# Rotary embedding and q·kᵀ in fp32 on one core: the last eight rows of five GpSimd loads move to other DMA engines

## The chip, the cores and the metric

The kernel runs on one core of a Trainium2 chip. The metric is device time in microseconds (us) of one execution. The core has a tensor engine (PE, with its weight loads shown as PEld), a vector engine (DVE), a scalar engine (ACT), GpSimd (POOL), and SyncE (SP), which here only issues transfers. Sixteen DMA engines move data between HBM and the on-chip memory; the code numbers them 0 to 15, and so does this text (E0 to E15).

## The reference

Inputs are `q` and `k` of shape (16, 512, 16, 64) in fp32 (batch, sequence, heads, dimension) and `cos`, `sin` of shape (512, 32). Both `q` and `k` are rotated, then multiplied for each position and each head of one batch against all positions of the same batch and head:

```python
q_rot = np.concatenate([q1 * cos_q - q2 * sin_q, q1 * sin_q + q2 * cos_q], axis=-1)
k_rot = np.concatenate([k1 * cos_q - k2 * sin_q, k1 * sin_q + k2 * cos_q], axis=-1)
scores = np.einsum('bshd,bthd->bsht', q_rot, k_rot)
```

`q1`, `q2` are the first and second half of the 64 columns, and `cos_q`, `sin_q` are spread over batch and heads. The output has shape (16, 512, 16, 512): 268.4 MB are written, 67.2 MB read.

## The kernel before

A batch of `q` or `k` is 512 positions of 1024 numbers (16 heads of 64). It is laid in a tile of 128 partitions ("rows" below), four positions to a row, so a row is 16 KB and a batch 2 MB. `in_pool` has two buffers for `q` and two for `k`. The work goes in 64 steps, four to a batch (`i // 4` is the batch). In step `i`, for each of eight pairs of heads, PE makes the scores of 128 positions against 512 (line 201), ACT copies them from PSUM to the tile `st` (line 208), and after the eighth pair SP stores `st`, 4 MB, to `out` (line 188). Three buffers `st` rotate. Beside it DVE rotates the next positions of `q` and `k` in place (lines 149, 150, 154), PE transposes them through PSUM (line 170), and DVE or ACT copies them out (line 185).

Batch 0 and the first loads come in smaller pieces (the tile `early`). From step 4 on the kernel loads whole batches: at the end of each step with `i % 4 == 2` the `q` of the next batch but one, at the end of each with `i % 4 == 3` the `k` of the batch three ahead, in `load` (lines 113 to 122). Most loads are one transfer of 128 rows of 16 KB that SP issues (line 122), between its stores, so that each DMA engine gets eight rows.

Five loads go around one DMA engine: those named in `RELIEVED`, `q` of batches 6, 11 and 15 and `k` of batches 7 and 12. `SLOW = 4` names the engine that is passed over. GpSimd issues their first 120 rows (line 98) as descriptors that are dealt out from a cursor: fifteen engines from E5 on, round to E3, get eight rows each, in two halves of 8 KB (the access pattern takes the second half first, so that a row stays two pieces). The cursor stands where the last GpSimd transfer left it; it is reset once (line 101) and moved by tiny reads into `scratch` of as many rows as the cursor is to move (`move_cursor`, line 84). The last eight rows go in one of two ways. For the three loads of `q`, SP issues them (line 111) as eight rows of 16 KB, one to each of E0 to E7. For the two loads of `k`, GpSimd issues them first (line 98, called from line 107), with the cursor at 8, so one row to each of E8 to E15.

The order of each engine's instructions is the order in which they are written. GpSimd does nothing else after the first microseconds: its transfers wait for the tile to come free (PE's last transpose from it), and, as eight completion semaphores go round among GpSimd's transfers, a transfer also waits until the one eight places before it has landed.

Of the kernel before, what the change touches and what calls it, by code (L numbers as in the profile page):

```python
# [10 lines left out]
def kernel(  # L11
# [8 lines left out]
    nc = tc.nc  # L20
    fp32 = mybir.dt.float32
# [3 lines left out]
    B, S, H, D = q.shape  # L25
    HD = D // 2
    P = 128
# [5 lines left out]
    const_pool = ctx.enter_context(tc.tile_pool(name="const", bufs=1))  # L33
# [37 lines left out]
    batches = {}  # L71

    RELIEVED = {("q", 6): 0, ("k", 7): 1, ("q", 11): 2, ("k", 12): 3, ("q", 15): 4}
    SLOW = 4
    scratch = const_pool.tile([P, 96], fp32, name="scratch")
    tiny = [0]

    def move_cursor(n):

        y = tiny[0]
        tiny[0] += 1
        src = bass.AP(q.tensor, 512 * y, [(512, n), (64, 2), (1, 2)])
        nc.gpsimd.dma_start(scratch[:n, 4 * y : 4 * y + 4].rearrange("p (a b) -> p a b", a=2), src)

    def load_around(which, b, t):

        n, E, F = 120, C * H * D, C * H * D // 2  # L90
        x = RELIEVED[which, b]
        d = dram[which][b]

        def halves(lo, hi):
            src = bass.AP(d.tensor, d.offset + lo * E + F, [(E, hi - lo), (-F, 2), (1, F)])
            v = t[lo:hi].rearrange("p c e -> p (c e)")
            dst = bass.AP(v.tensor, v.offset + F, [v.ap[0], (-F, 2), (1, F)])
            nc.gpsimd.dma_start(dst, src)  # L98

        if x == 0:  # L100
            nc.gpsimd.inc_swdge_sem([], [], mode="reset_dge_cursor")
        else:

            move_cursor(16 - SLOW)
        if x % 2:
            move_cursor(8)
            halves(n, P)
        move_cursor(SLOW + 1)
        halves(0, n)
        if not x % 2:  # L110
            nc.sync.dma_start(t[n:].rearrange("p c (h d) -> p c h d", h=H), d[n:])

    def load(which, b):

        if b >= B:
            return
        t = in_pool.tile([P, C, H * D], fp32, tag=which + "_in", name=which + "_sb")
        batches[which, b] = t
        if (which, b) in RELIEVED:
            load_around(which, b, t)  # L120
        else:
            nc.sync.dma_start(t.rearrange("p c (h d) -> p c h d", h=H), dram[which][b])
# [100 lines left out]
    with tc.manual_schedule():  # L223
# [15 lines left out]
        for i in range(C):  # L239
# [7 lines left out]
            for p in range(HP):  # L247
# [7 lines left out]
                if p in (2, 6):  # L255
                    m = len(dve) - (4 if p == 2 else 2) - (2 if i == C - 1 else 0)
# [64 lines left out]
```

## Time and profile before

| | |
|---|---|
| median of 4 runs | 792.83 us (791.71 to 793.74) |
| the profiled execution | 792.68 us |
| its span, first to last instruction | 790.9 us |
| mean granted PE clock | 0.936 |
| busy share of PE / ACT / DVE / POOL | 86% / 71% / 69% / 2% |
| moved by SP's queue (q1) | 325.46 MB in 16704 packets |
| moved by GpSimd's queue (q0) | 10.10 MB in 1808 packets |

The profile page gives the busy time of each engine and, for the DMA engines, the mean share of time that their packets took. The trace keeps more than the page: every packet with start, duration, size and queue (not the DMA engine that carried it), and every increment of a transfer's semaphore. A transfer raises its semaphore sixteen times, once as each engine ends its part, so the sixteen times of one transfer show how far apart the engines are. The engines work off SP's transfers in the order in which they were issued. As an engine's next packet starts within some nanoseconds of the end of the one before, the packets can also be strung together into sixteen chains, one for each engine.

### The profile page before, as it was taken

The page shows a single profiled execution, that of the slowest core. Times are in us where ns is not written, and L with a number is a line of the kernel's source. Part 1 is how long each engine was busy: PE and PEld are TensorE (multiplying, and loading weights), DVE is VectorE, ACT ScalarE, POOL GpSimd, SP SyncE. Part 2 cuts the span into 40 slices and gives each one's busy share as a digit, 9 for nine tenths or more (in the row PEclk, how much of TensorE's full clock was granted, in tenths as well). Part 3 has the DMA queues.
Part 4 walks back from the last instruction along what each step waited for, and adds up shares of the span by engine and source line. Part 5 has one row for each costly group of instructions (what it writes and reads, how often), then busy time and mean ns, then how long its engine had stood idle before and what let it go on. Part 6 is the DMA issues. An engine that isn't in the chain of part 4 may idle for free.

```text
span 790.9 us, 7750 instructions
## 1 busy us (share of the span) xinstructions
PE 683.9 (86%) x3072; PEld 295.0 (37%) x3072; DVE 544.5 (69%) x516; ACT 561.1 (71%) x647; POOL 12.0 (2%) x24
## 2 busy tenths in 40 slices
PE   4999998997989989798897978989899698799960
PEld 2444443343433434343343433334343243344420
DVE  7999987576865778575785856767678477587400
ACT  3888886785857778486785856768587586588770
POOL 0000000000001000000000001000000000000000
PEclk9999999898998999899998989999899899899995
DMA  9999999999999999999999999999999999999997
GB/s 358 419 426 438 428 438 429 423 441 431 427 427 430 421 432 411 439 423 432 440 423 434 437 427 426 424 430 430 430 431 424 439 433 427 426 435 428 433 435 315
DMA packets 18836, 336.18 MB, mean 425 GB/s; under 512 B 2312, under 2 KB 3592, under 8 KB 4616
## 3 DMA queue, kind: packets, MB, share of 16 engines
q1 hardware_dynamic: 16704, 325.46, 96.3%
q0 software_dynamic: 1808, 10.10, 3.1%
q8 instruction: 24, 0.39, 0.2%
q10 hardware_dynamic: 288, 0.13, 0.1%
q14 instruction: 12, 0.10, 0.0%
HBM read 67.24 MB, written 268.44 MB: 424 GB/s over the span
## 4 chain that ended last, share of the span: by engine, by line
DMA 46%; PE 38%; DVE 7%; ACT 5%; issue 1%; ACTq 0%
DMA out_dram<-st 46%; PE ps L201 29%; PE bank L170 9%; ACT st L208 5%; DVE part L149 2%; DVE early L150 1%; DVE early L154 1%; DVE k_sb L154 1%; DVE k_sb L150 1%; DVE kT_t L185 0%; DMA sin_t<-in_sin_dram 0%; DVE q_sb L150 0%; DVE q_sb L154 0%; ACTq L316 0%; DVE qT_t L185 0%
## 5 line engine op out<-in xcount | busy, mean ns | idle before, releaser
L208 ACT COPY st<-ps 128x1024 f32<-128x1024 f32 x512 | 495.0, 1020 | 194.4 <-DMA out_dram<-st 111.9
L201 PE MATMUL ps<-kT_t,qT_t 64*128 64x512 f32 x2048 | 542.6, 646 | 68.8 <-ACT st L208 68.7
L201 PEld LDWEIGHTS ps<-kT_t,qT_t 64*128 64x128 f32 x2048 | 181.6, 195 | 258.0 <-issue 133.8
L185 DVE COPY qT_t<-bank 128x512 f32<-128x512 f32 x118 | 81.6, 692 | 196.0 <-PE bank L170 196.0
L170 PEld LDWEIGHTS bank<-ident,q_sb 128*128 128x128 f32 x480 | 54.9, 150 | 102.2 <-issue 98.9
L170 PE MATMUL bank<-ident,q_sb 128*128 128x128 f32 x480 | 85.9, 306 | 0.8 <-PE ps L201 0.8
L170 PEld LDWEIGHTS bank<-ident,k_sb 128*128 128x128 f32 x480 | 50.3, 140 | 93.7 <-issue 38.0
L170 PE MATMUL bank<-ident,k_sb 128*128 128x128 f32 x480 | 78.6, 287 | 1.2 <-DVE qT_t L185 1.2
L185 ACT COPY kT_t<-bank 128x512 f32<-128x512 f32 x122 | 72.4, 598 | 6.2 <-PE bank L170 6.2
L150 DVE TENSOR_TENSOR q_sb<-q_sb,cos_t 128x1024 f32<-128x1024 f32 x60 | 73.5, 1225 | 2.1
L154 DVE TENSOR_TENSOR k_sb<-k_sb,part 128x1024 f32<-128x1024 f32 x60 | 73.5, 1225 | 2.1
L150 DVE TENSOR_TENSOR k_sb<-k_sb,cos_t 128x1024 f32<-128x1024 f32 x60 | 73.5, 1225 | 2.0
L149 DVE TENSOR_TENSOR part<-q_sb,ss_t 128x1024 f32<-128x1024 f32 x60 | 73.5, 1225 | 2.0
L149 DVE TENSOR_TENSOR part<-k_sb,ss_t 128x1024 f32<-128x1024 f32 x60 | 73.0, 1216 | 0.1
L154 DVE TENSOR_TENSOR q_sb<-q_sb,part 128x1024 f32<-128x1024 f32 x60 | 73.0, 1216 | 0.0
L170 PE MATMUL bank<-ident,early 128*128 128x128 f32 x64 | 10.5, 316 | 12.1 <-DVE early L154 10.1
L170 PEld LDWEIGHTS bank<-ident,early 128*128 128x128 f32 x64 | 8.3, 161 | 17.1 <-issue 13.0
L149 DVE TENSOR_TENSOR part<-early,ss_t 128x1024 f32<-128x1024 f32 x8 | 9.8, 1223 | 5.5 <-ACT ss_t L233 5.3
L98 POOL DMA_DIRECT2D q_sb<-in_q_dram x3 | 2.3, 754 | 619.3 <-PE bank L170 619.3
L154 DVE TENSOR_TENSOR early<-early,part 128x512 f32<-128x512 f32 x16 | 10.3, 687 | 0.2
L150 DVE TENSOR_TENSOR early<-early,cos_t 128x1024 f32<-128x1024 f32 x8 | 9.8, 1225 | 0.3
L185 ACT COPY qT_t<-bank 128x512 f32<-128x512 f32 x10 | 5.7, 628 | 3.1 <-PE bank L170 3.1
(12 smaller groups left out, 15.9 us busy)
## 6 DMA issues: line engine op xcount, KB each, us to landing
out_dram<-st SPq DMA_DIRECT2D x60, 4096.0 KB, 25.0
k_sb<-in_k_dram SPq DMA_DIRECT2D x13, 2048.0 KB, 27.7
q_sb<-in_q_dram SPq DMA_DIRECT2D x12, 2048.0 KB, 27.5
out_dram<-st SPq DMA_DIRECT2D x16, 1024.0 KB, 14.2
q_sb<-in_q_dram POOLq DMA_DIRECT2D x3, 1920.0 KB, 28.6
k_sb<-in_k_dram POOLq DMA_DIRECT2D x2, 1920.0 KB, 41.0
early<-in_k_dram SPq DMA_DIRECT2D x1, 1536.0 KB
early<-in_q_dram SPq DMA_DIRECT2D x1, 1536.0 KB
```

What stands on the lines that cost most here:

```text
L98: nc.gpsimd.dma_start(dst, src)
L149: nc.vector.tensor_tensor(pv, xs, ss, op=mult)
L150: nc.vector.tensor_tensor(xc, xc, cs, op=mult)
L154: nc.vector.tensor_tensor(y, y, z, op=add)
L170: nc.tensor.transpose(bank[:, x, :], src, ident)
L185: copy(out=dst, in_=src)
L201: nc.tensor.matmul(out=po, lhsT=lhs[64 * r : 64 * r + 64, :], rhs=rh, start=True, stop=True)
L208: nc.scalar.copy(out=so, in_=si)
```

## The change

The first 120 rows of each of the five loads go as before. Of the last eight rows none is issued by SP any more. For the loads of `q` they become two GpSimd transfers of four rows behind the 120 rows: one row each to E6 to E9, then one row each to E15, E0, E1 and E2. For the loads of `k` they stay one GpSimd transfer of eight rows ahead of the 120, but to E5 to E12 in place of E8 to E15. The cursor's place is now kept in the list `cursor`, and `rows` works out how far it has to move; where it has to move by one, two moves of nine and eight rows are made.

```diff
-    RELIEVED = {("q", 6): 0, ("k", 7): 1, ("q", 11): 2, ("k", 12): 3, ("q", 15): 4}
-    SLOW = 4
-    scratch = const_pool.tile([P, 96], fp32, name="scratch")
+    SPREAD, PACKED = (((6, 4), (15, 4)), False), (((5, 8),), True)
+    RELIEVED = {("q", 6): SPREAD, ("k", 7): PACKED, ("q", 11): SPREAD, ("k", 12): PACKED, ("q", 15): SPREAD}
+    SLOW, NE = 4, 16
+    scratch = const_pool.tile([P, 224], fp32, name="scratch")
     tiny = [0]
+    cursor = []
...
-        def halves(lo, hi):
+        def rows(lo, hi, engine):
+            d_n = (engine - cursor[0]) % NE
+            for m in (9, 8) if d_n == 1 else (d_n,) if d_n else ():
+                move_cursor(m)
             src = bass.AP(d.tensor, d.offset + lo * E + F, [(E, hi - lo), (-F, 2), (1, F)])
             v = t[lo:hi].rearrange("p c e -> p (c e)")
             dst = bass.AP(v.tensor, v.offset + F, [v.ap[0], (-F, 2), (1, F)])
             nc.gpsimd.dma_start(dst, src)
-
-        if x == 0:
+            cursor[0] = (engine + min(hi - lo, NE - 1)) % NE
+
+        if not cursor:
             nc.gpsimd.inc_swdge_sem([], [], mode="reset_dge_cursor")
-        else:
-
-            move_cursor(16 - SLOW)
-        if x % 2:
-            move_cursor(8)
-            halves(n, P)
-        move_cursor(SLOW + 1)
-        halves(0, n)
-        if not x % 2:
-            nc.sync.dma_start(t[n:].rearrange("p c (h d) -> p c h d", h=H), d[n:])
+            cursor.append(0)
+        parts, ahead = RELIEVED[which, b]
+
+        def last_rows():
+            lo = n
+            for engine, count in parts:
+                rows(lo, lo + count, engine)
+                lo += count
+
+        if ahead:
+            last_rows()
+        rows(0, n, SLOW + 1)
+        if not ahead:
+            last_rows()
```

In the built program GpSimd issues 28 transfers where it issued 18 (15 of the 28 are moves of the cursor, 11 of the 18), and SP issues 3 fewer. No other engine's order of instructions changes. As there are more GpSimd transfers, the one eight places ahead of a given transfer is another: the 120 rows of `k` of batches 7 and 12 now stand eight places behind the 120 rows of `q` of batches 6 and 11, and wait for their landing. Before, batch 7's had none ahead of it, and batch 12's had batch 7's, landed long ago.

More of the change, by code (lines that the diff above doesn't have):

```diff
@@ L90, in load_around @@
         n, E, F = 120, C * H * D, C * H * D // 2
-        x = RELIEVED[which, b]
         d = dram[which][b]
-        def halves(lo, hi):
+        def rows(lo, hi, engine):
+            d_n = (engine - cursor[0]) % NE
+            for m in (9, 8) if d_n == 1 else (d_n,) if d_n else ():
+                move_cursor(m)
             src = bass.AP(d.tensor, d.offset + lo * E + F, [(E, hi - lo), (-F, 2), (1, F)])
```

## The prediction

> **What bounds the kernel now.** I read the page's slices and DMA queues first, then its groups and ACT's waits, then the semaphore times and packets of single transfers.
>
> ```profile
> span 790.9 us, 7750 instructions
> ...
> DMA  9999999999999999999999999999999999999997
> ...
> q1 hardware_dynamic: 16704, 325.46, 96.3%
> q0 software_dynamic: 1808, 10.10, 3.1%
> ...
> L208 ACT COPY st<-ps 128x1024 f32<-128x1024 f32 x512 | 495.0, 1020 | 194.4 <-DMA out_dram<-st 111.9
> ...
> out_dram<-st SPq DMA_DIRECT2D x60, 4096.0 KB, 25.0
> ```
>
> The DMA engines are full in all slices but the last. ACT waits 111.9 us for stores to land, so compute is ahead, and a store lands 25.0 us after its issue, more than two stores' worth of work. Strung together, the packets leave no gap on any engine: each engine's end is the sum of what it carried. The span ends with the slowest of sixteen. So only who carries what counts, and the last store, issued at 768.40, shows who is late. Its first increment comes at 783.24; the sixteen in us after that:
>
> ```
> 0.00 0.08 0.58 0.92 1.45 3.67 3.77 3.80 3.82 4.32 4.46 4.48 4.61 4.69 6.43 6.64
> ```
>
> The last comes at 789.88, one us before the span's end. The mean is 3.36: perfect balance would gain 6.64 - 3.36 = 3.3 us, which bounds any such change. Two engines stand 1.7 to 2.0 us behind the third-last.
>
> The one at 6.43 is E4, the engine passed over. On it a 32 KB packet takes 1.246 to 1.255 us through most of the run; on the others 1.213. It is known by its packets during a 120-row load: between each two packets of 32 KB the other engines carry one of 8 KB, it carries one of 4 bytes (16 of them from 673.27 to 692.23). That these shares fall on fifteen engines shows that cursor moves of 5, 8 and 12 work as the code counts.
>
> The one at 6.64 I call X. At 574 us its lag was 5.62; it went to 7.11 at 594 to 601, where one 16 KB packet of the instruction queue (596.87, 0.96 us) delayed an engine, and stayed last. Such packets (24 in the run) hit several engines; X is late by chance of where they fall, E4 by its nature. Is X in reach of SP's eight rows?
>
> ```profile
> 674.73 0.33 SPq L188 DMA_DIRECT2D out_dram<-st  x1
> 675.16 1.10 SPq L111 DMA_DIRECT2D q_sb<-in_q_dram  x1
> ```
>
> The store of 674.73 has increments from 696.05 to 702.77. The eight-row load behind it has nine: one at once, eight from 696.68 to 701.14, each at least 0.6 us behind one of the store's, none behind 702.77. So X is not among E0 to E7. E4 is: in its chain a single 16 KB packet of 0.611 us stands at 699.12.
>
> **The change part by part.** A row costs its engine 0.61 us (16 KB packet 0.611; two of 8 KB, 0.309 each, the same).
>
> Rows. Before, E0 to E7 carry three last rows (three loads of `q`), E8 to E15 two (two of `k`). After: E0 to E2 three, E3 and E4 none, E5 two, E6 to E9 five, E10 to E12 two, E13 and E14 none, E15 three. So E4 loses 3 x 0.61 = 1.83 us: 789.67 to 787.84. X changes by 0 (E10 to E12), -1.22 (E13, E14), +0.61 (E15) or +1.83 (E8, E9); nothing in the trace tells which of the eight it is. The third-last, at 787.93, stays if it is not one of E6 to E9, and else comes to 789.15 or 789.76.
>
> Tiny packets. An engine without rows gets packets of 4 bytes in their place, so E4 has two for each of six four-row transfers, and some for the cursor moves; about 12 new ones in the three loads of `q`. In the load of 668.39 the first eight left the 32 KB packets about as they were (1.22 to 1.27), the last eight came with 1.412 to 1.495, some 0.2 to 0.245 more. Bounds 0 and 12 x 0.245 = 2.9 us; in the moves around 257 to 265, the nearest row, most 32 KB packets stay at 1.213, so I take 0.4 us. The engines near the end get as much.
>
> GpSimd's issue. A transfer takes 0.57 us (eight rows) to 0.76 us (120); ten more are 6 us on an engine busy 2%. Behind the wait for batch 6's `q` stand the `k` loads (GpSimd's timeline, then DVE's):
>
> ```profile
> 248.37 0.57 POOL L98 DMA_DIRECT2D k_sb<-in_k_dram  x1 [19.38 <-PE bank L170]
> 248.93 0.57 POOL L84 DMA_DIRECT2D scratch<-in_q_dram  x1
> 249.50 0.76 POOL L98 DMA_DIRECT2D k_sb<-in_k_dram  x1
> ```
>
> ```profile
> 289.65 0.69 DVE L185 COPY qT_t<-bank 128x512 f32<-128x512 f32 x1 [4.50 <-PE bank L170]
> 290.26 1.22 DVE L149 TENSOR_TENSOR part<-k_sb,ss_t 128x1024 f32<-128x1024 f32 x1
> ```
>
> The 120 rows of `q` issued at 227.10 landed at 256.45, so the issue of 249.50 moves to about 256.5, 7 us later. It landed at 289.80, and DVE uses it at 290.26: no margin. But GpSimd's queue is worked off in order, and the eight rows of `k` ahead of it landed only at 264.33, so its packets hardly began before; I take 1 us later landing, bounds 0 and 7. Behind DVE's wait stand `q`'s rotation and copies for PE, so compute may be up to 7 us late, twice (batch 12: landing 535.05, use 536.29, issue 493.34 against 501.17). The cover: at 290 the engines still hold the store of 282.07 (lands 305.36), the load of 282.50 (311.14), and at 296.05 the next store comes. 15 us of work in hand, so nothing reaches the end; without that cover it would be up to 14 us.
>
> `q`'s last rows. They now follow the 120 on GpSimd's queue: two packets, each behind one of 32 KB, 2 x (1.213 + 0.309) = 3.0 us after 256.45, about 259.5; SP's landed at 262.46, DVE needs them at 268.81. Nothing. SP loses 1.10 to 1.29 us of issue at three places where its next instruction waits some 15 us for ACT: nothing.
>
> The sum. E4 ends at 787.84 + 0.4 = 788.2. If X is relieved it ends at 789.88 - 1.22 + 0.4 = 789.1, else at 789.9 to 790.3. In executions where the instruction packets fall otherwise, X is not there, and the gain is what separates E4 from the next engines, 1.0 to 1.7. I take -0.9 us for the span, against the profiled 792.68 (1.8 us around the span), and as the median is 0.15 above it: 792.83 - 0.9 = 791.9.
>
> The Trainium skill has two rules against it. "DMA: Bandwidth & Descriptors", section "Rules for kernel authors", says that spreading transfers over several issuing engines brings no bandwidth: by it the move from SP to GpSimd is worth 0, 792.8; the trace agrees on the queue, and only the choice of engine is priced above. The same page, section "Latency and other measured facts", calls engines 7 and 15 usually the slower ones under GpSimd's descriptors; here the slow one is E4, but if the rule held for the last engine, E7 (+2 rows) or E15 (+1) would put 0.6 to 1.2 us on the end, 793.4 to 794.0.
>
> **The rivals.**
>
> A (main): E4 is relieved and the end passes to an engine 0.2 to 1.8 us earlier, 791.0 to 792.6. For it: E4 is late in every part of the run. Against: X.
>
> B: X stays where it is, or tiny packets eat E4's relief (above half of the 2.9 us). Time 792.8 to 793.7. For it: three of eight places for X get no change.
>
> C (slower): one of E8, E9 is the last or within 1.8 us of it, and gets three rows more. From an increment of 4.9 in the list above it decides; for X itself 789.88 + 1.83 + 0.4 = 792.1, a time of 795.1; from 4.69, 789.8 + 0.4, no loss. Against: five engines are early by 5 us or more, and any of those has room for +1.83.
>
> D: the cursor is not where the code counts it, since moves of 2 and 9 and transfers of 4 do not occur in the trace. From the first miscount E4 gets eight rows, 4.9 us, of each later 120-row load: with four of them, 19.6 - 1.8, about 810; with one 796.
>
> **How the numbers follow.** 0.2% of 792.83 is 1.6 us, about what a measurement can tell from no change. A has 0.64 (of it 0.36 below 791.24, as runs scatter by 0.25%, and 0.28 within 0.2%), B 0.18 (0.12 within, 0.06 slower), C 0.14 (slower), D 0.04 (slower). Faster 0.36, same 0.40, slower 0.24. The time is A's, 791.9. Range: from 790.0, the full 1.95 us down to the third-last and a low run, to 794.5, which takes B and half of C; A alone is 790.6 to 792.9.
>
> **What would show it.** Right: no line of SP's at `q`'s last rows; the last store's latest increment is not E4's; the spread of its sixteen is below 6.64. Wrong: E4's 4-byte packets slow their neighbours (1.4 us and more) at every four-row transfer; the last engine carries 8 KB packets behind the 120 rows (E8, E9); 8 KB packets on E4 (D); ACT's waits for stores fall while DVE waits for `k_sb` (the late 120 rows were not covered).

## The result, and the profile after

| | before | after |
|---|---|---|
| median | 793.03 us (791.71 to 795.07, 60 runs) | 794.05 us (793.14 to 795.37, 42 runs) |
| the profiled execution | 792.68 us | 794.79 us |
| its span | 790.9 us | 792.7 us |

The ratio after to before is 1.0013, with a 95% interval of 1.0008 to 1.0017. The changed kernel is 1.0 us slower. That is less than the 0.2% which the prediction called no change, and inside its range, but the forecast was a gain of 0.9 us, and the interval leaves no room for a gain. Taken once more later (e15), the ratio was 1.0010, 1.0002 to 1.0019.

The page of the changed kernel, in the parts that were shown of before:

```profile
span 792.7 us, 7758 instructions
...
DMA  9999999999999999999999999999999999999997
...
q1 hardware_dynamic: 16656, 325.07, 96.0%
q0 software_dynamic: 2224, 10.49, 3.2%
...
L216 ACT COPY st<-ps 128x1024 f32<-128x1024 f32 x512 | 494.6, 1020 | 187.2 <-DMA out_dram<-st 107.6
...
L157 DVE TENSOR_TENSOR part<-k_sb,ss_t 128x1024 f32<-128x1024 f32 x60 | 73.0, 1216 | 26.1 <-DMA k_sb<-in_k_dram 25.9
...
out_dram<-st SPq DMA_DIRECT2D x60, 4096.0 KB, 24.9
...
k_sb<-in_k_dram POOLq DMA_DIRECT2D x2, 1920.0 KB, 42.3
```

The rows went where the diff says: SP's queue lost 0.39 MB, which is 24 rows of 16 KB, and GpSimd's queue gained it. The DMA engines are as full as before, and ACT waits 107.6 us for stores to land instead of 111.9: compute has lost some of its lead but still waits for the engines. New on the page is DVE's idle time of 25.9 us before it rotates `k`. `k`'s 120 rows land 42.3 us after their issue (41.0 before), but they are issued 8 us later. So the end is again the slowest of sixteen engines, and each of them ends when it has carried what it carries.

The last store's sixteen increments after its first (784.99 us):

```
0.00 0.28 0.38 0.86 1.40 2.07 2.36 2.38 2.55 3.21 3.69 3.80 4.50 5.09 5.90 6.51
```

The spread is 6.51 us where it was 6.64 (in a second profile of each, below, 7.21 and 7.01), and the first comes 1.75 us later. The rows were dealt out anew and the engines are no better balanced, and all sixteen are late together.

Both can be read off the packets strung into sixteen chains. Two profiles of each kernel are to hand (the second from e0 and e15). These executions are not median ones: they took 792.68 and 793.85 us before, 794.79 and 796.11 after, so the pairs lie 2.2 us apart where the medians lie 1.0 apart. The table, called the ledger below, gives the end of the last 32 KB packet on each engine, and the time an engine lost, in us per engine on the mean of the sixteen: packets of 32 KB above 1.213, packets of 16 and 8 KB above 0.611 and 0.309, packets under 512 bytes, gaps between packets, and packets of instructions.

| | before | e0 (before) | after | e15 (after) |
|---|---|---|---|---|
| mean end of the sixteen | 786.24 | 786.57 | 787.44 | 787.73 |
| latest end | 789.55 | 790.57 | 791.16 | 792.47 |
| E4's end | 789.20 | 790.57 | 789.61 | 790.50 |
| lost: 32 KB packets | 2.62 | 2.53 | 2.71 | 2.73 |
| lost: 16 and 8 KB packets | 1.86 | 1.99 | 2.58 | 2.83 |
| lost: packets under 512 bytes | 1.22 | 1.23 | 1.41 | 1.41 |
| lost: gaps | 0.05 | 0.01 | 0.21 | 0.22 |
| lost: instructions | 1.66 | 1.65 | 1.63 | 1.63 |
| lost in all | 7.42 | 7.40 | 8.54 | 8.81 |

The sixteen end 1.2 us later on the mean (787.59 against 786.41), and the ledger says what that is: 0.78 us in slow packets of 16 and 8 KB, 0.18 in the packets under 512 bytes that the ten more transfers bring, 0.18 in gaps, and the rest in 32 KB packets. The two profiles of each kernel agree within 0.3 us. One execution can lie further off: those of e9 and e14 below lost 9.23 and 8.45 us at medians like that of before, and the sixteen of e9 end at 788.25 on the mean, later than in either profile of after. So the 1.2 us is a reading of two executions against two, and it is not shown that the change causes it. Most of the slow packets stand in two places, SP's loads of `q` for batches 7 and 12: 0.63 and 0.10 us per engine before (0.76 and 0.27 in e0), 0.81 and 0.72 after (0.77 and 0.68 in e15). These two loads hold 0.61 of the 0.78. SP's loads from 50 to 226 us, ahead of GpSimd's first load, lost 0.26 and 0.32 us before, 0.27 and 0.90 after, although the two programs issue the same instructions up to there. In the two loads nearly all engines read slowly at the same time, above all in the last four of their eight rows.

What else became late is plain in two views of the changed kernel. First GpSimd's timeline (start, duration, engine, line, operation, tile, and in brackets the idle time before it and what ended it):

```profile
246.75 0.57 POOL L101 DMA_DIRECT2D k_sb<-in_k_dram  x1 [15.34 <-PE bank L178]
247.32 0.56 POOL L87 DMA_DIRECT2D scratch<-in_q_dram  x1
257.59 0.76 POOL L101 DMA_DIRECT2D k_sb<-in_k_dram  x1 [9.71 <-DMA q_sb<-in_q_dram]
```

The 120 rows then come too late for DVE, in its timeline around batch 7:

```profile
285.38 0.69 DVE L193 COPY qT_t<-bank 128x512 f32<-128x512 f32 x1 [2.58 <-PE bank L178]
300.68 1.23 DVE L157 TENSOR_TENSOR part<-k_sb,ss_t 128x1024 f32<-128x1024 f32 x1 [14.61 <-DMA k_sb<-in_k_dram]
```

And the waits of the same kernel (engine, tile and line, what it waited for, us in all, times, longest):

```profile
DVE part L157 <- DMA k_sb<-in_k_dram: 25.9, 2, 14.6
DVE part L157 <- DMA q_sb<-in_q_dram: 0.6, 1, 0.6
POOL k_sb L101 <- DMA q_sb<-in_q_dram: 18.3, 2, 9.7
```

The issue of `k`'s 120 rows waits 9.7 us for the landing of `q`'s, as forecast (257.59 where 256.5 was said). But the 120 rows land at 300.60 and not at 290.8: 10.8 us later than before, and 8.5 us later for batch 12 (543.6 against 535.0). DVE waits 25.9 us in all for them. The landing times of GpSimd's transfers in order show why. Before, and after:

```
before  q 120: 256.45  move: 258.87  move: 260.09  k 8: 264.33  move: 266.76  k 120: 289.80
after   q 120: 257.30  move: 258.90  q 4: 262.99  move: 265.40  q 4: 268.05  move: 270.27  k 8: 274.51  move: 276.93  k 120: 300.60
```

GpSimd's transfers land in order. In these two rows a move, some tens of bytes, takes 1.2 to 2.4 us of the queue, a transfer of four or eight rows 2.6 to 4.2, and the 120 rows 23 to 24 from the landing ahead of them. Between the two loads of 120 stood four transfers; now there are seven. The way from the landing of `q`'s 120 rows to that of the last transfer ahead of `k`'s takes 19.6 us where it took 10.3. The wait at the issue is not what counts: at 257.59 the queue has 19 us of work ahead. The Trainium skill ("DMA: Bandwidth & Descriptors", section "Rules for kernel authors") advises to gather many small transfers into a large one because small ones cost mostly overhead. These rows agree, with 1.2 to 2.4 us for a move.

### The profile page after: what moved, and what is told of

Its sections match the earlier page's. It is cut to its first block, busy times and chain, and to the rows that moved or that the text cites. A ratio compares the mean times of both kernels' runs of the same rounds, so it can differ in the third digit from the quotient of the medians.

```text
span 792.7 us, 7758 instructions
## 1 busy us (share of the span) xinstructions
PE 681.5 (86%) x3072; PEld 294.5 (37%) x3072; DVE 544.1 (69%) x516; ACT 561.1 (71%) x647; POOL 17.8 (2%) x34
## 2 busy tenths in 40 slices
DMA packets 19204, 336.18 MB, mean 424 GB/s; under 512 B 2656, under 2 KB 3936, under 8 KB 4960
## 4 chain that ended last, share of the span: by engine, by line
DMA 55%; PE 28%; DVE 9%; ACT 4%; issue 1%; ACTq 0%; DVEq 0%
DMA out_dram<-st 36%; PE ps L209 21%; DMA k_sb<-in_k_dram 11%; DMA q_sb<-in_q_dram 7%; PE bank L178 7%; ACT st L216 4%; DVE part L157 3%; DVE early L158 1%; DVE k_sb L162 1%; DVE k_sb L158 1%; DVE early L162 1%; DVE q_sb L158 1%; DMA sin_t<-in_sin_dram 0%; DVE kT_t L193 0%; DVE q_sb L162 0%
## 5 line engine op out<-in xcount | busy, mean ns | idle before, releaser
L216 ACT COPY st<-ps 128x1024 f32<-128x1024 f32 x512 | 494.6, 1020 | 187.2 <-DMA out_dram<-st 107.6
L157 DVE TENSOR_TENSOR part<-k_sb,ss_t 128x1024 f32<-128x1024 f32 x60 | 73.0, 1216 | 26.1 <-DMA k_sb<-in_k_dram 25.9
L101 POOL DMA_DIRECT2D q_sb<-in_q_dram x9 | 5.8, 647 | 596.7 <-PE bank L178 596.7
L162 DVE TENSOR_TENSOR early<-early,part 128x512 f32<-128x512 f32 x16 | 10.3, 687 | 0.2
L87 POOL DMA_DIRECT2D scratch<-in_q_dram x15 | 8.7, 580 | 8.5 <-DMA q_sb<-in_q_dram 6.4
## 6 DMA issues: line engine op xcount, KB each, us to landing
k_sb<-in_k_dram POOLq DMA_DIRECT2D x2, 1920.0 KB, 42.3
```

The lines of the kernel that those rows point to most:

```text
L157: nc.vector.tensor_tensor(pv, xs, ss, op=mult)
L162: nc.vector.tensor_tensor(y, y, z, op=add)
L216: nc.scalar.copy(out=so, in_=si)
```

## The experiments

Each was timed in five rounds beside the kernel before. Ratios are to before, with 95% intervals.

| run | edit | median, us | ratio |
|---|---|---|---|
| e0 | before, unchanged | 793.40 | 0.9997 (0.9988 to 1.0006) |
| e1 | q's last rows by GpSimd, to E0 to E7 | 793.91 | 1.0008 (0.9999 to 1.0016) |
| e2 | three idle moves ahead of k's loads | 794.14 | 1.0007 (0.9998 to 1.0016) |
| e3 | three idle moves behind them | 794.02 | 1.0008 (1.0000 to 1.0017) |
| e4 | after, q's rows off E6 to E9 | 794.10 | 1.0007 (0.9999 to 1.0016) |
| e5 | after, k's 120 rows ahead of its 8 | 796.90 | 1.0045 (1.0033 to 1.0058) |
| e6 | e4 and e5 | 795.89 | 1.0037 (1.0024 to 1.0049) |
| e7 | before, SP's eight rows as two loads of four | 794.02 | 1.0012 (1.0003 to 1.0021) |
| e8 | after, q's eight rows in one transfer | 794.19 | 1.0008 (0.9999 to 1.0017) |
| e9 | before, SP's loads of q 8 and 13 later | 793.29 | 0.9995 (0.9986 to 1.0004) |
| e10 | e8 and e9 | 794.81 | 1.0017 (1.0008 to 1.0026) |
| e11 | after and e9 | 794.31 | 1.0011 (1.0002 to 1.0020) |
| e12 | before, SP's loads of q 7 and 12 later | 793.24 | 0.9990 (0.9982 to 0.9999) |
| e13 | after and e12 | 793.85 | 1.0002 (0.9993 to 1.0011) |
| e14 | before, GpSimd's loads one batch earlier | 793.25 | 0.9995 (0.9986 to 1.0004) |
| e15 | after, unchanged | 794.54 | 1.0010 (1.0002 to 1.0019) |
| e16 | e12, unchanged | 792.82 | 0.9994 (0.9985 to 1.0003) |
| e17 | e12, SP's eight rows in halves | 793.28 | 0.9998 (0.9990 to 1.0007) |

The intervals are 1.4 us wide, so most single runs do not tell 0.5 us from nothing. Where a verdict is drawn from a trace, it is said.

One more thing differs between these kernels, beside the edits shown. The tile `scratch`, into which the moves of the cursor read, is 96 columns wide in before, e0, e7, e9, e12, e14, e16 and e17, 224 in after, e1 to e4, e8, e10, e11, e13 and e15, and 256 in e5 and e6. It stands in the kernel's first pool, so the tiles of `q`, `k` and `st` lie 512 or 640 bytes further on in each partition where it is wider. The ratios go with the width: 0.9990 to 0.9998 at 96 columns, except e7 with 1.0012; 1.0002 to 1.0017 at 224; 1.0037 and 1.0045 at 256. No run widens `scratch` and does nothing else. So the place of the tiles is a rival to every cause discussed below, and it was not tested.

### Is there a difference at all: e0 and e15

e0 is the kernel before and e15 the changed one, each without an edit.

> The kernel before, unchanged, entered as if it were a variant. It shows what the comparison gives for no change at all and a second profile of before. If the variants so far are really slower by 0.6 to 1.0 us, this one comes out at a ratio of 1.0000 +- 0.0007 and its ledger of time lost by the DMA engines is near the 7.42 us of the first profile. If the comparison or the submitted place itself costs something, it shows 1.0005 or more; if the ledger's differences are mere scatter between executions, its ledger lies at 8 to 8.5 us, with a median like before's.

> The changed kernel once more, unchanged, with a second profile. If the time lost per DMA engine tells the two kernels apart and not merely two executions, the ledger is again 8.2 to 8.9 us against before's 7.42 and 7.40, the two slow loads of q have 0.5 us or more each, the extra tiny packets and gaps are again near 0.35 us, and the ratio is 1.0008 to 1.0018; the last engines are among E6 to E9 again.

e0 came out at 0.9997 with a ledger of 7.40 us (7.42 in the first profile); e15 at 1.0010 with 8.81 (8.54). So the comparison is not biased, and the changed kernel is slower. e0 also shows that the engine I called X in the first profile was a chance: here E4 alone is last, 1.27 us behind the next.

In e15 the engines can be told by their 8 KB packets in the third load of `q`, where the first four of the last rows come near 701 us and the second four near 707. The four engines with the first four rows, E6 to E9, end at 785.79, 785.94, 790.79 and 792.47: two of them are the last two of all, later than E4 at 790.50. In the first profile of the changed kernel the last two (790.53 and 791.16) read as two of E6 to E9 as well, though there two chains seem to have changed places once and the reading is less sure. So E4's place at the end has been taken by engines that got two rows more (E6, E7: 1.22 us) or three (E8, E9: 1.83 us). Which of the four the last two are, the trace does not tell.

### The rows, and who issues them: e1, e4, e7, e17

e1 leaves `q`'s last rows on E0 to E7 and has GpSimd issue them, with no more transfers than before between the loads of 120:

```diff
-            nc.sync.dma_start(t[n:].rearrange("p c (h d) -> p c h d", h=H), d[n:])
+            move_cursor(16 - SLOW)
+            halves(n, P)
```

> Before, with one edit: the last eight rows of the q loads are issued by GpSimd, one row to each of E0 to E7 as SP did, and no transfer waits for one in flight. Rows per DMA engine are unchanged. Theory L (the end is set by the rows that E6 to E9 got): no change, 0 +- 0.4 us, end of the last store as before. Theory W (the late 120 rows of k cost it): no change, since k's 120 rows are issued at once. Theory P (each extra GpSimd transfer costs every engine some time): two transfers more, at most +0.1 us. Theory I (rows issued by GpSimd cost more than rows issued by SP): +0.5 to +1 us.

Time 1.0008, not told from no change. In the trace E4 is last, 2.3 us behind the next engine (791.78 and 789.53), as it may be without relief, and `k`'s 120 rows land at 294.1, since a move in the queue became a transfer with rows. The Trainium skill's rule quoted in the prediction, that another issuing engine brings no bandwidth, is not contradicted: the issuer alone gains nothing.

e4 is the changed kernel with the rows taken off E6 to E9:

```diff
-    SPREAD, PACKED = (((6, 4), (15, 4)), False), (((5, 8),), True)
+    SPREAD, PACKED = (((15, 4), (0, 4)), False), (((5, 8),), True)
```

> After, with the rows of q that went to E6 to E9 going to E0 to E3 (so E15 three rows, E0 to E2 six, E3 three, E6 to E9 two). The waits and the number of transfers stay, with one move more per q load. L: the engines that end last in the changed kernel lose 1.83 us each, E4 is last, 792.0 to 793.0 us, 1 to 1.7 us under the changed kernel. W and P: no gain, 794.0 us or a little over.

The spread of the last store falls from 6.51 and 7.21 us (after, e15) to 5.58, and the latest end lies 2.6 us above the mean where it lay 3.7 and 4.7 above it. So the balance was mended. The time did not show it: 1.0007, and the sixteen end at 787.56 on the mean, as in the changed kernel.

e7 relieves E4 without GpSimd: SP's load of eight rows becomes two of four.

```diff
-            nc.sync.dma_start(t[n:].rearrange("p c (h d) -> p c h d", h=H), d[n:])
+            for lo in (n, n + 4):
+                nc.sync.dma_start(t[lo : lo + 4].rearrange("p c (h d) -> p c h d", h=H), d[lo : lo + 4])
```

> The kernel before with one edit: SP's load of q's last eight rows is issued as two loads of four rows, which go to E0 to E3 twice if a load of SP's starts at the lowest engine as the load of eight did. No GpSimd transfer, move or wait is added. E4 loses 1.83 us in the three loads, E0 to E3 gain as much. If E4's lateness sets the end, its increment of the last store falls from the last two places by 1.8 us and the time falls by 0.3 to 1.5 us (0.9980 to 0.9996). If the end is set by whichever engine happens to be delayed, nothing shows: 0.9996 to 1.0004.

E4 was relieved: it ends at 784.42, 2.9 us before the mean, fourth of the sixteen. And the kernel was not faster but slower, 1.0012. The trace shows who ends last instead. The last eight rows of the third load are carried by four engines, two rows each, from 700.51, 701.15, 702.64 and 703.22. After them nine stores follow, so each of the four still carries 72 packets of 32 KB; strung on from there, they are the engines that end at 788.86, 789.50, 791.41 and 791.57. The last two are the last two of all. These four are the ones to which the edit gave three rows more, 1.83 us each, in place of E4 to E7. The ledger rose to 8.20, but not by slow loads: the packets of 16 and 8 KB lost 1.90 us, as before, though around 258 us several of 16 KB took 1.3 to 2.8 us instead of 0.611, and those of 32 KB lost 3.33. By the same count E4 would have ended near 786.3 without the edit, and the last two near 789.7: an estimate, by which E4 was not the last in this execution to begin with. So this run, with GpSimd's part and `scratch` as before, speaks most plainly against my sum: taking rows off E4 is not worth its lag, because E4 is not the last in every execution and the rows fall on engines that may stand later.

e17 is e12 (below) with SP's eight rows as sixteen halves of 8 KB:

```diff
-            nc.sync.dma_start(t[n:].rearrange("p c (h d) -> p c h d", h=H), d[n:])
+            halves(n, P, nc.sync)
```

> e12 with SP's load of q's last eight rows in sixteen halves of 8 KB instead of eight rows of 16 KB. If SP's sixteen pieces go to sixteen engines, E0 to E7 lose 0.92 us each in the three loads and E8 to E15 gain as much, with no more GpSimd work: E4's increment of the last store comes 0.9 us earlier against the mean, and the time falls by 0 to 0.9 us against e12 if E4 is last there, and rises by as much if one of E8 to E15 is. If both halves of a row stay on one engine, as on GpSimd's queue, nothing changes.

The load still raised its semaphore nine times, as the whole rows did, so it still used eight engines. Nothing was relieved, and 0.9998 says no more.

### The late rows of k: e2, e3, e5, e6, e8

e2 puts three idle moves into the kernel before, between the 120 rows of `q` and `k`'s loads; e3 puts the same moves behind `k`'s loads, with `(1, 3)` for `(0, 2)`:

```diff
         halves(0, n)
+        if x in (0, 2):
+            for m in (8, 4, 4):
+                move_cursor(m)
```

> Before, with three idle cursor moves (8, 4 and 4 rows, together one turn of 16) behind the 120 rows of q of batches 6 and 11. They push the 120 rows of k of batches 7 and 12 to eight places behind those of q, so that they wait for their landing as in the changed kernel. Rows per DMA engine are unchanged. W: DVE waits some 26 us for k_sb, the loads of 16 KB rows around 305 and 551 us are slowed on many engines, +0.6 to +1 us. L: DVE's wait appears, the time stays, 0 +- 0.4 us. P: six tiny transfers more, +0.2 us.

> Before, with the same six idle moves, but behind the 120 rows of k, so that k's 120 rows wait for nothing in flight. Rows unchanged. P: +0.2 us or more, as much as in the run with the moves ahead of k. W: 0 here, and the difference between the two runs is the wait's price. L: 0 +- 0.3 us in both.

e2's `k` lands at 297.1 and 542.4, e3's at 291.3 and 535.0. Their waits, e2 first:

```profile
DVE part L152 <- DMA k_sb<-in_k_dram: 20.6, 2, 10.5
POOL k_sb L98 <- DMA q_sb<-in_q_dram: 15.4, 2, 8.0
```

```profile
DVE part L152 <- DMA k_sb<-in_k_dram: 3.4, 2, 2.4
```

DVE waits six times as long in e2. The load of `q` for batch 12 loses 0.75 us per engine in e2 and 0.22 in e3, but that for batch 7 0.90 and 0.99. So only the second of the two slow loads goes with the late rows of `k` here, and e9 (below) loses 0.93 us in it with `k` in time (535.6). The times do not tell them apart, 1.0007 and 1.0008, and both lie where the changed kernel lies: six moves that carry nothing and hardly delay `k` seem to cost as much, though e3's interval reaches to 1.0000, and the wider `scratch`, which both have, could cost it too.

e5 tried to mend the lateness by sending `k`'s 120 rows ahead of its eight; e6 does so with the rows of e4.

```diff
-    SPREAD, PACKED = (((6, 4), (15, 4)), False), (((5, 8),), True)
+    SPREAD, PACKED = (((6, 4), (15, 4)), False), (((5, 8),), False)
```

> The changed kernel with the 120 rows of k issued ahead of k's last eight rows; rows, their engines and q's part unchanged, one GpSimd transfer more per load of k. The 120 rows of k then no longer wait for the 120 rows of q. Theory W (the late 120 rows of k cost the microsecond): k's 120 rows of batch 7 are issued near 249.5 and land near 290, DVE's wait for k_sb falls from 25.9 us to under 8, and the time falls back to before's, ratio 1.0000 (0.9994 to 1.0005). Theories L (rows on E6 to E9) and P (more GpSimd transfers): as the changed kernel, 1.0010 to 1.0015.

> The changed kernel with both corrections: q's last rows at E15, E0 to E2 and E0 to E3, and k's 120 rows ahead of its eight. E4 still carries no row of any of the five loads. W plus L: spread of the last store's increments at 5 to 5.6 us, no wait for k_sb, time under before, 0.9985 to 1.0000. P (what counts is the number of GpSimd transfers, here 12 more than before): 1.0008 to 1.0015 whatever the spread.

My expectation of both failed. The 120 rows were issued at 249.14 in e5, but the eight rows now come behind them, and with two moves (for a step of one), the second of which waits for `q`'s 120 rows. GpSimd's timeline and the waits of e5:

```profile
249.14 0.76 POOL L101 DMA_DIRECT2D k_sb<-in_k_dram  x1 [17.25 <-PE bank L178]
249.90 0.57 POOL L87 DMA_DIRECT2D scratch<-in_q_dram  x1
257.99 0.57 POOL L87 DMA_DIRECT2D scratch<-in_q_dram  x1 [7.53 <-DMA q_sb<-in_q_dram]
260.42 0.57 POOL L101 DMA_DIRECT2D k_sb<-in_k_dram  x1 [1.85 <-DMA scratch<-in_q_dram]
```

```profile
DVE part L157 <- DMA k_sb<-in_k_dram: 28.4, 2, 15.6
```

The last of `k` lands at 302.0 and 550.6, later than in the changed kernel (300.6 and 543.6), and the second time in the middle of SP's load of `q` (549 to 560). That load then loses 1.21 us per engine, and the one at 303 us 1.37. The ledger of e5 is 11.19 us, of e6 10.27, most of the rise in 16 and 8 KB packets (4.62 and 4.15), and the times are 3.6 and 2.6 us above before. These two are the runs whose time moves clearly. But late rows of `k` cannot be all of it: from 50 to 226 us, ahead of GpSimd's first load, SP's loads lost 1.38 us per engine in e5 and 1.86 in e6, where all other runs lost 0.26 to 1.02. Up to there these two issue the same instructions as the changed kernel (0.27, and 0.90 in e15), and what differs is the width of `scratch`. How the slow reading goes with the compute around it, the windows around the second load show (length in us; busy time and instructions of PE, PEld, DVE, ACT and POOL; granted clock; share of the DMA engines' time; GB/s). Before, then after, then e5:

```profile
545.00:555.00 10.00, 10.00 (x50) 4.43 (x48) 8.53 (x9) 8.67 (x11) 0.00 (x0) 1.00 1.02 433
```

```profile
545.00:555.00 10.00, 6.96 (x32) 3.10 (x32) 9.83 (x10) 5.15 (x7) 0.00 (x0) 0.95 0.97 383
```

```profile
545.00:555.00 10.00, 3.63 (x16) 1.41 (x16) 4.14 (x4) 4.76 (x6) 0.00 (x0) 0.92 0.98 365
```

The DMA engines are busy in all three (1.02, 0.97, 0.98), so they do not starve, while PE's busy time falls from 10.00 to 6.96 and 3.63 of 10 us, and what the engines move from 433 to 383 and 365 GB/s. The two do not hang together, though. The same window in e9, where `k` is in time, and in e11, where it is as late as in the changed kernel:

```profile
545.00:555.00 10.00, 10.00 (x51) 4.43 (x48) 8.01 (x8) 9.04 (x12) 0.00 (x0) 1.00 0.98 380
```

```profile
545.00:555.00 10.00, 5.27 (x21) 1.96 (x18) 9.76 (x10) 3.82 (x5) 0.00 (x0) 0.85 0.99 416
```

PE is busy throughout in e9 while the engines move only 380 GB/s, and half idle in e11 while they move 416. The loss of e5 is in slower packets and not in a missing store: its gaps are 0.28 us per engine of its 11.19. How much of it the late `k` brings is not separated from the width of `scratch`.

e8 puts `q`'s eight rows into one transfer, so that five transfers stand between the loads of 120 instead of seven, and none waits for `q`'s 120 rows:

```diff
-    SPREAD, PACKED = (((6, 4), (15, 4)), False), (((5, 8),), True)
+    SPREAD, PACKED = (((12, 8),), False), (((6, 8),), True)
```

> The changed kernel with each of q's two transfers of four rows replaced by one of eight (E12 to E15 and E0 to E3), and k's eight at E6 to E13. E4 still carries none, k's 120 rows no longer wait for q's 120 (they are the eighth GpSimd transfer, not the tenth), and there are two transfers fewer per pair of loads. Theory W (the late 120 rows cost the time, through the slowed load of q behind them): k's 120 rows land near 294 instead of 300.6, DVE's wait for k_sb falls from 25.9 to about 7 us, time lost per DMA engine falls from 8.5 to 7.4 to 7.8 us, and the time is at or under before's, ratio 0.9985 to 1.0003. Theory P (anything more that GpSimd carries costs): 1.0006 to 1.0012, as all variants so far.

`k`'s 120 rows land at 295.1 and 539.6, and DVE's waits for DMA are less than half of those after:

```profile
DVE part L157 <- DMA k_sb<-in_k_dram: 11.7, 2, 5.9
```

But the loads of `q` lost 0.84 and 0.89 us all the same, the ledger is 8.10, and the time 1.0008. Half the lateness was gone and no gain can be told.

Over the runs, the landing of batch 7's 120 rows of `k` follows the number of transfers between the two loads: 289.8 to 292.4 with four, of them one with rows (before, e0, e3, e7, e9, e12, e16, e17), 294.1 with four, two of them with rows (e1), 293.4 and 295.1 with five (e10, e8), 297.1 to 300.6 with seven (e2, after, e11, e13, e15), 303.4 with eight (e4). The slow reading follows only loosely. For batch 12, over the fifteen runs in which its load stands where it did: `k` landed before 536 us, 0.10, 0.27, 0.22, 0.03 and 0.93 us per engine (and e14 moved away); 538 to 540, 0.12, 0.89, 0.78; 542 to 545, 0.72, 0.75, 0.35, 0.19, 0.68; 549 and later, 1.21, 0.71. The means are 0.31, 0.60, 0.54 and 0.96.

### Where the slow reading comes from: e9 to e14, e16

Theory S held that a load which SP issues while `k`'s 120 rows are under way is read slowly. e9, e10 and e11 were to move these loads one store later:

```diff
+            late = i // C + 2 in (8, 13)
-            if i % C == C - 2:
+            if i % C == (C - 1 if late else C - 2):
                 load("q", i // C + 2)
-            elif i % C == C - 1:
+            if i % C == C - 1:
                 load("k", i // C + 3)
```

> The kernel before with SP's loads of q for batches 8 and 13 moved one store later (issued just ahead of k's load, near 296 instead of 282.5). Theory S (a load that SP issues while GpSimd's 120 rows of k are still under way is read slowly, which is what the late rows of k make worse): the excess of these two loads, 0.6 to 0.8 and 0.1 to 0.3 us per engine in two profiles of before, falls under 0.1 each, and the time falls by 0.4 to 1.0 us, 0.9987 to 0.9996. If the slow reading belongs to the place of the data or to the compute at that time, the excess stays at 0.6 or moves to k's load, and the time stays (0.9996 to 1.0004).

> e8_q8 with the loads of q for batches 8 and 13 one store later. If both W and S hold, the lowest of all: lost time per engine 6.6 to 7 us, E4 not last, ratio 0.9970 to 0.9992. If neither holds, as e8_q8.

> The changed kernel, late 120 rows of k and all, with the loads of q for batches 8 and 13 one store later. Theory S: the excess of the two loads (0.81 and 0.72 us per engine in the changed kernel) goes to under 0.1 each though DVE still waits 25 us for k_sb, and the time falls by about 1.4 us against the changed kernel, to a ratio of 0.9985 to 0.9998 against before. If the slow reading is caused by DVE's late work and not by the load's own place in the queue, the excess stays and the ratio is 1.0010 to 1.0015.

I had counted the batches wrongly: the load of 282.5 is batch 7's, and these runs moved the load of 333. They show nothing of S. As further executions they show the scatter: e9, with GpSimd's part of before, lost 0.93 us per engine in the load of batch 12, and e11, with that of the changed kernel, 0.19. e12 and e13 name `(7, 12)` instead:

> The kernel before with SP's loads of q for batches 7 and 12, the two that the profiles show to be read slowly, moved one store later (e9 and its like had moved batches 8 and 13, one batch too far). Theory S (a load issued by SP while GpSimd's 120 rows of k are under way is read slowly): the excess of these two loads, 0.63 to 0.76 and 0.10 to 0.27 us per engine in two profiles of before, falls under 0.1 each, and the time by 0.4 to 1.0 us, ratio 0.9987 to 0.9996. If the place of the data or chance makes them slow: excess 0.5 and more stays in one of them, ratio 0.9996 to 1.0005.

> The changed kernel with the same move of the loads of q for batches 7 and 12. Theory S: its excess of 0.81 and 0.72 us falls under 0.1 each though DVE still waits some 25 us for k_sb, time 1.0 to 1.4 us under the changed kernel, ratio to before 0.9992 to 1.0000. Otherwise 1.0008 to 1.0016 as the changed kernel.

SP's timeline of e12 shows the load behind the next store, back to back with `k`'s:

```profile
271.13 27.16 SPq L188 DMA_DIRECT2D out_dram<-st  x3
298.39 1.19 SPq L122 DMA_DIRECT2D q_sb<-in_q_dram  x1
299.69 1.17 SPq L122 DMA_DIRECT2D k_sb<-in_k_dram  x1
```

DVE now waits for `q`, 12.6 us in all:

```profile
DVE part L149 <- DMA q_sb<-in_q_dram: 12.6, 2, 6.9
```

The load of `q` is now read at full speed (0.01 and 0.00 us lost in e12, 0.00 and 0.02 in e13), so its place decides. But the load of `k` behind it took over the slow reading, 0.67 and 0.39 us in e12, 0.48 and 0.68 in e13, again in the last four of its rows. Before, that load was clean (0.07 and 0.10). So S as I put it is wrong: issue under the 120 rows is not the condition, since `k`'s load of 299.69 was issued after they had landed (291.2). The times fell a little: e12 0.9990, and e13 1.0002 beside e15's 1.0010 on the same chip.

e14 moves GpSimd's loads one batch earlier:

```diff
-    RELIEVED = {("q", 6): 0, ("k", 7): 1, ("q", 11): 2, ("k", 12): 3, ("q", 15): 4}
+    RELIEVED = {("q", 5): 0, ("k", 6): 1, ("q", 10): 2, ("k", 11): 3, ("q", 15): 4}
```

> The kernel before with the GpSimd loads one batch earlier (q of 5 and 10, k of 6 and 11; q of 15 stays). Theory S: the slow loads move with them, to SP's loads of q for batches 6 and 11, excess 0.3 to 0.8 us together, and batches 7 and 12 are read at 0.00 to 0.05; time as before, 0.9995 to 1.0005. If the place of the data in memory makes 7 and 12 slow, they stay slow.

Batches 7 and 12 were then read at 0.03 and 0.00 us, so the place of these batches in HBM is not the cause, and the loads of 6 and 11, which now follow GpSimd's, lost 0.14 and 0.11, less than expected. Its 32 KB packets lost 3.47 us instead of 2.6. The time stayed, 0.9995. What slows nearly all engines' reads together, in the loads that follow GpSimd's, was not found. Nor are these loads alone in it: a load of SP's between 72 and 163 us, ahead of GpSimd's first, lost 0.37 to 0.68 us per engine in e5, e6, e9, e11, e15 and e17.

e16 repeats e12, as the one edit that seemed to help:

> e12 once more, unchanged (the kernel before with the loads of q for batches 7 and 12 one store later). If it is a real gain, its ratio is again 0.9985 to 0.9998; if the 0.9990 of e12 was the edge of its interval, 0.9996 to 1.0004.

0.9994 (0.9985 to 1.0003), a ledger of 7.36. Both runs lie below before, only the first interval leaves out 1. If moving the two loads gains anything over the kernel before, it is about half a microsecond, and that is not settled.

## Why the prediction went wrong

1. *The DMA engines are full, and the end is the slowest of sixteen.* Right, and still so after.
2. *E4 loses 1.83 us.* The rows are gone from it as counted. Against the mean of the sixteen it lies 2.2 and 2.8 us late after, 3.0 and 4.0 before: about 1 us better, with a scatter of 1 us.
3. *X is late by chance.* Right: e0 does not have it. But the sum measured the room behind E4 in one profile only, and gave two more rows to E6 and E7 and three to E8 and E9, with a chance of 0.14 that it matters (rival C). It did: two of these four end last in e15. My own sentence had the size, "and else comes to 789.15 or 789.76": the last two increments after are 790.89 and 791.51, which less the 1.2 us that all engines are late is 789.7 and 790.3. The case A, that the end passes to an engine 0.2 to 1.8 us earlier, failed.
4. *Tiny packets, 0.4 us.* The mean of the sixteen rose by 0.18 us, less than half of that; E4 alone was not measured.
5. *The late 120 rows of k, 1 us, bounds 0 and 7.* Wrong, 10.8 and 8.5 us. I let the eight rows of `k` that land at 264.33 stay where they were, and moved only the issue behind them. Between the landing of `q`'s 120 rows and those eight stood two moves, 3.6 us; now there are five transfers, 13.0 us, and the eight rows landed at 274.51. What a transfer costs its queue stood in the landings of before, and I did not read it there.
6. *q's last rows about 259.5.* The same mistake: 262.99 and 268.05. DVE waited 0.6 us for them, once; the margin of 9 us was gone.
7. *15 us of work in hand, so nothing reaches the end.* For compute this held though the lateness was ten times what I took: the DMA engines' gaps rose by 0.18 us only. But work in hand was the only cover I asked for, and packets that take longer were put at nothing. In the profiles every engine ends 1.2 us later on the mean, 0.61 of it in two loads of `q` that follow GpSimd's. No term of the sum could hold that; whether the change is its cause is open.

The step that failed is the last one, from E4's rows to the time. The sum let the end fall by "what separates E4 from the next engines", as if those stayed where they were. But the rows had to go to others: in e15 two of E6 to E9, with two or three rows more, end at 790.79 and 792.47 behind E4's 790.50, and in e7 two of E0 to E3, with three rows more, end at 791.41 and 791.57 behind E4's 784.42. Nor is E4 the last in every execution.

That is not all of it. The sum was -0.9; what came was +1.0. In e4, with the rows off E6 to E9, the last engine stands 2.6 us above the mean, where it stood 3.3 and 4.0 above it before, and the time is still no better, 1.0007. So something else takes back the gain, and its cause stays open: the late `k`, the ten transfers themselves, or the wider `scratch`. e3, with moves but `k` hardly late, e8, with half the lateness, and e1, with only two transfers more, all come out at 1.0008, and all three have the wider `scratch`.

Of the signs named beforehand, all three of being right came true in the first profile of after: no line of SP's at `q`'s last rows, E4 not the last, a spread below 6.64. They did not tell a gain from a loss, and the spread's sign was chance (7.21 in e15). Of the signs of being wrong, two came true: ACT's waits for stores fell while DVE waited for `k_sb`, and the last engines carry 8 KB packets behind the 120 rows.

## What to carry to other kernels

When every DMA engine is full, a change that relieves one engine can gain no more than that engine's lag behind the next, less what the engines that take its work lose by it. Both must be read from several executions: who stands second changes from one to the next. Count a queue by its transfers and not by its bytes or its issue times: each transfer put ahead, however small, delays all behind it, and the landings of its neighbours in the trace give the price. Full DMA engines can still move less, so compare what they move in a stretch, not only whether they are busy. And keep everything else in place: when a variant needs a wider tile, time the kernel before with that tile too, or the place of the tiles stays a rival.

## What the runs showed of the hardware that was not expected

- SP's loads of 128 rows that follow GpSimd's loads were read slowly by nearly all DMA engines at once: 16 KB packets of 0.7 to 2.1 us instead of 0.611, and in the runs that leave these loads in place 0.14 to 1.37 us lost per engine in the first such load, 0.03 to 1.21 in the second. The same load one store later is clean and the next load is slow in its place. Single loads ahead of GpSimd's first were slow too, by up to 0.68 us (e6).
- SP's small loads of `q`'s last rows can be slow as well: packets of 1.3 to 2.8 us on some engines in e7, where they are two loads of four rows, but also up to 2.09 us in e14 and 1.37 in e9, where they are one of eight.
- An engine that has no row in a GpSimd transfer still gets packets of 4 bytes (16 of them on E4 during a load of 120 rows): the page counts 2656 packets under 512 bytes after, 2312 before, for ten transfers more.
